# State space mixer of a two-layer trunk: its pieces in another order, convolution one chunk at a time, other engines for the first splits

## Chip, cores and metric

One core of a Trainium2 chip runs one launch of the kernel. The metric is the device time of a launch in microseconds (us), median of three runs; the profile is one further execution.

## What is computed

The reference is a trunk of two layers on 256 tokens of width 1024, in fp32. Layer 0 is a Mamba-2 mixer, layer 1 a retention; each is followed by a product-key expert network (the long part: 16384 expert rows of `peer_u` and `peer_v`) and a gated input embedding. Only the mixer of layer 0 is touched by the order of the change:

```python
proj = h @ w_in                                   # 1024 -> 2048 (z) + 3072 (x, B, C) + 32 (dt)
z = proj[..., :DI]
xbc = silu(causal_depthwise_conv(proj[..., DI:DI + 3072], conv_w, conv_b))   # 4 taps
dt = softplus(proj[..., DI + 3072:] + dt_bias)
# chunked scan: y[t] = sum_s exp(cum_t - cum_s) * (C_t . B_s) * dt_s * x_s, plus the state of the chunks before
y = (y + d_skip * xs) * silu(z)
y = rms_norm(y in 4 groups of 512, norm_g)
return y @ w_out                                  # 2048 -> 1024
```

## The kernel before

**Layout.** Activations are transposed: a chunk is 128 channels on the partitions by 256 tokens. Each weight tile (128 x 1024) is loaded by SP (`load`), cast to a high part on ACT (`wh`, L133) and subtracted to a low part (`wl`, L136) on DVE, or on POOL where `eng=pool` says so; a matmul step (`Acc.step`, L199) runs 16 matmuls with wh and then 8 with wl. `raws` has four buffers for loads, `wsp` two for each of wh and wl. `makers` holds the weights in order; `begin` issues the next load, `prepare` splits the oldest load, and `get` hands a step its weight, prepares the next one and issues one more load. `prepare(True)` (by `ahead` in the mixer, and in `finish`) emits the cast and keeps the subtraction for later; with `eager` set, `get` emits it one step before its use. So the DVE queue holds, step by step, one subtraction and then what the step's pieces ask for.

**Stages of the mixer.** (1) Eight steps for B and C (columns group 4), with the input's norm run beside them by the plan `FIRST_SSD`, one string of letters for each step: a is nine small row loads, q the squares, t the total, s the spread of the root, c and b small parameters, 0/1 the scaling of each half of the normalised input on DVE, h/H its split (ACT cast L187, DVE subtraction L188). (2) Eight steps for x chunks 0 to 7 (group 2), with the convolution of B and C beside them. (3) dt's 24 matmuls, then eight steps for x chunks 8 to 15 (group 3), with the convolution of chunks 0 to 7 and dt's softplus (`dt_a`, `dt_b`, `dt_c`) beside them. (4, 5) Sixteen steps for z, evacuated after every eight by `z_evac` (L786 ACT tanh, L787 DVE). (6) Sixteen steps of w_out, fed by the four normalised groups.

**Order of the work around the steps.** After step k a dense loop emits a written number of entries of the list `todo` (`fill`). `SSD_ORDER` writes them for stages 4 to 6, one group between bars for each step. cpN is a piece of the convolution of chunks 8 to 15 (`conv_piece`: first tap on ACT L598, three more taps on DVE L593 for two chunks at once, later the silu L603 of two chunks). x{tb}{q} transposes four chunks on PE and scales them on DVE (L678, L679); X and Y make the part across halves (DVE L698; PE L702, DVE L703); uN, eN, hN belong to a pair of heads: masks on ACT (L710), cumulative sums on PE with exp on ACT and the product on DVE (L716, L718, L720), and the output (PE L730, L732, DVE L734). aN multiplies a group by its gate and squares it (DVE L747, ACT L284, POOL L285, L286), bN sums it (PE L249, DVE L256, POOL L258, DVE L268), cN spreads the root and splits the group (PE L275, DVE L301, ACT L302, DVE L295). cbN is C times B under the causal mask (PE L685, DVE L687).

All engines work through their queues in the order written. PSUM: `acc` four banks for the steps' sums, `mis` two (tiles m: cb, e, dt, and each group's sums from b to c), `gps` two (tiles g: x, Y, h).

Of the kernel before, what the change touches and what calls it, by code (L numbers as in the profile page):

```python
# [18 lines left out]
P = 128  # L19
T = 256  # L20
D = 1024
# [10 lines left out]
    cp0 x00 x10 u0 | cp1 X0 e0 u1 | cp2 Y0 e1 x01 x11 | cp3 h0 u2 X1 | cp4 e2 h1 u3 Y1 | cp5 e3 h2 u4  # L32
    | cp6 e4 h3 u5 x02 x12 | cp7 e5 h4 u6 a0
    | e6 h5 u7 b0 X2 | e7 h6 u8 x03 x13 | c0 e8 h7 u9 Y2 | a1 e9 h8 u10 | e10 h9 u11 b1 | e11 h10 u12 X3 c1
    | e12 h11 u13 Y3 | e13 h12 u14 a2
    | e14 h13 u15 | b2 e15 h14 | h15 | c2 a3 | | b3 | c3 | | | | | | | | |
# [3 lines left out]
SSD_DT = "dt_a dt_b dt_c cb0 edge cb1 cb2 cb3".split()  # L40
# [6 lines left out]
FIRST_SSD = ('aq', 't', 'c', 's', '0h', '', '1H', 'b')  # L47
# [38 lines left out]
def trunk(ctx: ExitStack, tc: tile.TileContext, a, out, dbg=None, stop=None):  # L86
# [43 lines left out]
    def split_r(r, n=D, eng=None):  # L130
        wh = wsp.tile([P, D], F32R, name="wh")
        wl = wsp.tile([P, D], F32R, name="wl")
        act.copy(wh[:, :n], r[:, :n])  # L133

        def lo():
            (eng or dve).tensor_sub(wl[:, :n], r[:, :n], wh[:, :n].bitcast(F32))  # L136
            return wh, wl

        return lo

    makers, begun, ready = [], [], []
    eager = [False]

# [10 lines left out]

    def get(more=True):
        if not ready:
            prepare()
        v = ready.pop(0)
        if callable(v):
            v = v()  # L160
        if ready and callable(ready[0]) and eager[0]:
            ready[0] = ready[0]()
        if more and not ready:
            prepare()
        begin()
        return v

    def staged(r, n, eng):
        return lambda: split_r(r, n, eng)

    def weights(w, n0, n1, k0=0, k1=KD, eng=None):
        for k in range(k0, k1):
            makers.append(lambda k=k: staged(load(w[k * P:(k + 1) * P, n0:n1], n1 - n0), n1 - n0, eng))
# [230 lines left out]
    def x_load(i):  # L404
        for tb in range(2):
            c = slice(512 * i, 512 * i + 512)
            sp.dma_start(xts[tb][:, c], a["x"][0, tb * P:(tb + 1) * P, c])

    x_load(0)
# [11 lines left out]
    row_load(*ROWS1[0], act)  # L421

# [60 lines left out]
    def total0():  # L483
        st0.sums = Sums()
        st0.dg = st0.sums.diag(D, ss, act)

    def before0(k):
# [3 lines left out]
        for b in (2 * k, 2 * k + 1):  # L491
            st0.hi(2 * b)
            st0.hi(2 * b + 1)
            if b == 0:
                prepare()
                begin()
# [38 lines left out]
    for g in (4, 2, 3):  # L535
        for k in range(KD):
            weights(a["ssd_w_in"][0], g * D, (g + 1) * D, k, k + 1, eng=pool if g == 4 and k else None)
# [21 lines left out]
    def ssd(st):  # L559
# [27 lines left out]
        def conv(c):  # L587
            r = rawc[c // 8]
            for m in range(1, 4):
                for j in range(2):  # L590
# [11 lines left out]
        def conv_silu(c):  # L602
            act.activation(xbc[:, c:c + 2], xbc[:, c:c + 2], AF.Silu)  # L603
# [8 lines left out]
        def conv_piece(c0, i):  # L612
            if i in (1, 2, 3, 4):
                conv(c0 + 2 * i - 2)
            if i >= 4:
                conv_silu(c0 + 2 * i - 8)
# [6 lines left out]
        xs = []  # L623
        begin()
# [31 lines left out]
        def dt_b():  # L656
# [5 lines left out]
            dve.tensor_mul(f4, f[3], f[3])  # L662
            dve.tensor_scalar(f[5], f4, 1.0 / 15, None, op0=OP.mult)
# [75 lines left out]
        def ahead():  # L739

            if len(ready) < 2:
                prepare(True)

# [15 lines left out]

        cp = conv_pieces(8)  # L760
        names = {"dt_a": (dt_a,), "dt_b": (dt_b,), "dt_c": (dt_c,), "edge": (edge,)}
        for i in range(8):
            names[f"cp{i}"] = cp[i]
# [13 lines left out]
        for c, n in zip(conv_pieces(0), SSD_DT):  # L777
            todo.extend((c, names[n]))
        dense(xs, conv_evac(8), lambda k: 2)
# [10 lines left out]
        eager[0] = True  # L790
# [12 lines left out]
        eager[0] = False  # L803
# [694 lines left out]
```

## Time and profile before

| | us |
|---|---|
| time, median of 3 runs (lowest to highest) | 2169.11 (2167.49 to 2170.3) |
| the profiled execution | 2167.4 |
| its span | 2165.6 |
| PE busy in the span | 2119.3 |
| mixer of layer 0, start of the span to its last step | 251.3 |

The profile is read from the stage: a table of busy times by stretch shows where PE stood and where its clock was low; the timeline of PE names for each wait the engine that ended it; the timelines of DVE, ACT and POOL at that place show what stood ahead of it in that engine's queue.

### The profile page before, as it was taken

The page shows a single profiled execution, that of the slowest core. Times are in us where ns is not written, and L with a number is a line of the kernel's source. Part 1 is how long each engine was busy: PE and PEld are TensorE (multiplying, and loading weights), DVE is VectorE, ACT ScalarE, POOL GpSimd, SP SyncE. Part 2 cuts the span into 40 slices and gives each one's busy share as a digit, 9 for nine tenths or more (in the row PEclk, how much of TensorE's full clock was granted, in tenths as well). Part 3 has the DMA queues.
Part 4 walks back from the last instruction along what each step waited for, and adds up shares of the span by engine and source line. Part 5 has one row for each costly group of instructions (what it writes and reads, how often), then busy time and mean ns, then how long its engine had stood idle before and what let it go on. Part 6 is the DMA issues. An engine that isn't in the chain of part 4 may idle for free. (4 is left out here: it accounts for less than half of the span.)

```text
span 2165.6 us, 39617 instructions
## 1 busy us (share of the span) xinstructions
PE 2119.3 (98%) x15013; PEld 1965.6 (91%) x15013; DVE 1553.3 (72%) x2638; ACT 1229.1 (57%) x2149; POOL 786.7 (36%) x365
## 2 busy tenths in 40 slices
PE   8989999999999999999999999999999999999997
PEld 8988999999999888888898999999999998888887
DVE  6767678888999555555686456989799975555556
ACT  5666444448887444444554444445688864444445
POOL 3001168886777100000133224788777740000001
PEclk9989999999999999999999999999999999999999
DMA  5423577655555665566656456765555566666653
GB/s 184 149 69 108 185 196 189 179 138 158 157 157 157 203 193 193 193 192 194 198 175 185 135 159 182 192 187 150 156 151 158 154 184 194 194 194 193 194 188 120
DMA packets 219574, 370.24 MB, mean 171 GB/s; under 512 B 24240, under 2 KB 163192, under 8 KB 219384
## 3 DMA queue, kind: packets, MB, share of 16 engines
q1 hardware_dynamic: 219064, 367.19, 57.0%
q8 instruction: 117, 1.92, 0.4%
q14 instruction: 73, 0.60, 0.1%
q10 hardware_dynamic: 320, 0.53, 0.1%
HBM read 364.48 MB, written 1.05 MB: 169 GB/s over the span
## 5 line engine op out<-in xcount | busy, mean ns | idle before, releaser
L136 DVE TENSOR_TENSOR wl<-raw,wh 128x1024 fp32r<-128x1024 f32 x398 | 496.5, 1249 | 401.4 <-ACT wh L133 401.2
L133 ACT CAST wh<-raw 128x1024 fp32r<-128x1024 f32 x429 | 450.5, 1051 | 480.0 <-PE ps L1309 358.3
L528 POOL TENSOR_TENSOR wl<-raw,wh 128x1024 fp32r<-128x1024 f32 x256 | 618.4, 2417 | 201.3 <-ACT wh L525 183.8
L1283 PE MATMUL m<-X,wh 128*128 128x256 f32 x2048 | 508.6, 286 | 1.1 <-ACT wh L525 1.0
L1309 PE MATMUL ps<-wh,X 128*128 128x512 f32 x2048 | 507.0, 389 | 0.0
L1284 PE MATMUL m<-X,wh 128*128 128x256 f32 x2048 | 502.2, 283 | 0.0
L1309 PEld LDWEIGHTS ps<-wh,X 128*128 128x128 f32 x2048 | 384.2, 188 | 79.5
L1283 PEld LDWEIGHTS m<-X,wh 128*128 128x128 f32 x2048 | 392.5, 192 | 2.2 <-ACT wh L525 1.9
L1284 PEld LDWEIGHTS m<-X,wh 128*128 128x128 f32 x2048 | 392.7, 192 | 0.0
L199 PE MATMUL ps<-X,wh 128*128 128x256 f32 x2368 | 334.2, 291 | 6.9 <-ACT wh L133 4.2
L344 POOL TENSOR_TENSOR arena<-arena 128x512 f32<-128x512 f32 x15 | 24.1, 1607 | 817.3 <-ACT arena L342 808.3
L199 PEld LDWEIGHTS ps<-X,wh 128*128 128x128 f32 x2368 | 306.4, 196 | 13.1 <-ACT wh L133 5.2
L1287 PE MATMUL m<-X,wl 128*128 128x256 f32 x2048 | 288.1, 283 | 2.0 <-POOL wl L528 1.9
L525 ACT CAST wh<-raw 128x1024 fp32r<-128x1024 f32 x256 | 266.7, 1042 | 24.1 <-DVE raw L520 15.2
L1309 PE MATMUL ps<-wl,X 128*128 128x512 f32 x1024 | 274.7, 389 | 0.0
L1287 PEld LDWEIGHTS m<-X,wl 128*128 128x128 f32 x2048 | 264.0, 192 | 3.8 <-POOL wl L528 3.8
L1309 PEld LDWEIGHTS ps<-wl,X 128*128 128x128 f32 x1024 | 192.2, 188 | 39.9
L1223 ACT ACTIVATE arena<-m 128x256 f32<-128x256 f32 (+15 forms) x248 | 82.2, 331 | 228.3 <-PE m L1287 227.9
L520 DVE STREAM_TRANSPOSE raw<-raw 128x1024 f32<-128x1024 f32 x144 | 179.0, 1243 | 41.1 <-DMA raw<-in_peer_u 31.1
L199 PE MATMUL ps<-X,wl 128*128 128x256 f32 x1184 | 176.7, 286 | 5.7 <-DVE wl L136 3.5
L199 PEld LDWEIGHTS ps<-X,wl 128*128 128x128 f32 x1184 | 157.6, 194 | 7.9 <-DVE wl L136 4.3
L520 DVE STREAM_TRANSPOSE raw<-arena 128x1024 f32<-128x1024 f32 x112 | 138.0, 1235 | 30.0 <-POOL wl L528 26.5
(269 smaller groups left out, 1992.0 us busy)
## 6 DMA issues: line engine op xcount, KB each, us to landing
raw<-in_peer_v SPq DMA_DIRECT2D x256, 512.0 KB, 4.3
raw<-in_peer_u SPq DMA_DIRECT2D x576, 128.0 KB, 3.1
arena<-in_peer_u SPq DMA_DIRECT2D x448, 128.0 KB, 3.3
raw<-in_ret_w_in SPq DMA_DIRECT2D x48, 512.0 KB, 4.0
raw<-in_ssd_w_in SPq DMA_DIRECT2D x41, 512.0 KB, 3.8
raw<-in_peer_w_q SPq DMA_DIRECT2D x32, 512.0 KB, 4.5
raw<-in_ssd_w_out SPq DMA_DIRECT2D x16, 512.0 KB, 3.9
raw<-in_ple_gate SPq DMA_DIRECT2D x16, 512.0 KB, 4.5
```

The costliest lines, as they stand in the source:

```text
L133: act.copy(wh[:, :n], r[:, :n])
L136: (eng or dve).tensor_sub(wl[:, :n], r[:, :n], wh[:, :n].bitcast(F32))
L199: pe.matmul(self.t[n // 2][:, n % 2], w[:, n * P:(n + 1) * P], x, start=st, stop=sp_, skip_group_check=True)
L344: pool.tensor_add(self.sq[:, 0], self.sq[:, 0], self.sq[:, b])
L520: dve.transpose(t.rearrange("p (k b i) -> p b k i", k=8, b=4), r.rearrange("p (b k i) -> p b k i", k=8, b=4))
L525: act.copy(wh, t)
L528: pool.tensor_sub(wl, t, wh.bitcast(F32))
L1223: act.activation(H[:, i, st:], ps[:, st:], AF.Gelu)
L1283: pe.matmul(last, wh[:, s], xh, start=k == 0, stop=False)
L1284: pe.matmul(last, wh[:, s], xl, start=False, stop=False)
L1287: pe.matmul(last, wl[:, s], xh, start=False, stop=k == KD - 1)
L1309: pe.matmul(sums[b], h[:, tb * P:(tb + 1) * P], w[:, n * 512:(n + 1) * 512], start=i == 0 and p == 0, stop=i == P - 1 and p == 2)
```

## The change

Loads at the start: the first halves of x go out after the row of gains, one on SP and one on ACT's queue; two weights are begun before the second halves of x, and the `begin` inside `before0` goes. The first weight of group 4 is cast on DVE instead of ACT; of group 4 only the second weight has its subtraction on POOL (before: the second to the eighth). `total0` calls `ahead` first. `FIRST_SSD` has the split of the first half one step later, the second half's scaling together with b and its split at the end. `get` always emits a kept subtraction one step ahead, in all stages of the kernel.

In the convolution, pieces for chunks 0 to 15 are now separate entries: F (first tap, two chunks), v (three taps of one chunk), S (silu of four chunks). dt's softplus is cut in two (`dt_b`, then `dt_B` for the series). Stage 3 has its own list by step, `SSD_DT`; cb2 and cb3 move from stage 3 to stages 4 and 5. In `SSD_ORDER` x11, x12, x03, x13 and the a, b and c entries come at other steps.

```diff
 SSD_ORDER = """
-    cp0 x00 x10 u0 | cp1 X0 e0 u1 | cp2 Y0 e1 x01 x11 | cp3 h0 u2 X1 | cp4 e2 h1 u3 Y1 | cp5 e3 h2 u4
-    | cp6 e4 h3 u5 x02 x12 | cp7 e5 h4 u6 a0
-    | e6 h5 u7 b0 X2 | e7 h6 u8 x03 x13 | c0 e8 h7 u9 Y2 | a1 e9 h8 u10 | e10 h9 u11 b1 | e11 h10 u12 X3 c1
-    | e12 h11 u13 Y3 | e13 h12 u14 a2
-    | e14 h13 u15 | b2 e15 h14 | h15 | c2 a3 | | b3 | c3 | | | | | | | | |
+    S4 x00 x10 u0 F8 | X0 e0 u1 v8 F10 | Y0 e1 x01 v9 F12 | h0 u2 X1 v10 F14 | e2 h1 u3 Y1 v11 | e3 h2 u4 x11 v12 S8
+    | e4 h3 u5 x02 v13 | e5 h4 u6 v14 cb2
+    | e6 h5 u7 X2 x12 v15 | a0 e7 h6 u8 S12 | e8 h7 u9 Y2 | b0 e9 h8 u10 x03 | e10 h9 u11 x13 cb3 c0
+    | a1 e11 h10 u12 X3 | e12 h11 u13 Y3 | b1 e13 h12 u14
+    | e14 h13 u15 c1 | e15 h14 a2 | h15 | b2 | a3 | c2 | | b3 | c3 | | | | | | |
 """
...
-SSD_DT = "dt_a dt_b dt_c cb0 edge cb1 cb2 cb3".split()
+SSD_DT = """
+    F0 F2 dt_a | F4 v0 dt_b | F6 v1 dt_B | v2 dt_c | edge v3 | S0 v4 cb0 | v5 cb1 | v6 v7
+"""
+SSD_DT = [p.split() for p in SSD_DT.split("|")]
...
-FIRST_SSD = ('aq', 't', 'c', 's', '0h', '', '1H', 'b')
+FIRST_SSD = ('aq', 't', 'c', 's', '0', 'h', '1b', 'H')
...
-    def split_r(r, n=D, eng=None):
+    def split_r(r, n=D, eng=None, cast=None):
...
-        act.copy(wh[:, :n], r[:, :n])
+        (cast or act.copy)(wh[:, :n], r[:, :n])
...
+    def ahead():
+
+        if len(ready) < 2:
+            prepare(True)
...
-        if ready and callable(ready[0]) and eager[0]:
+        if ready and callable(ready[0]):
             ready[0] = ready[0]()
...
-            sp.dma_start(xts[tb][:, c], a["x"][0, tb * P:(tb + 1) * P, c])
-
-    x_load(0)
+            (act if i == 0 and tb else sp).dma_start(xts[tb][:, c], a["x"][0, tb * P:(tb + 1) * P, c])
...
     row_load(*ROWS1[0], act)
+    x_load(0)
...
     def total0():
+        ahead()
...
             if b == 0:
                 prepare()
-                begin()
...
-            weights(a["ssd_w_in"][0], g * D, (g + 1) * D, k, k + 1, eng=pool if g == 4 and k else None)
+            weights(a["ssd_w_in"][0], g * D, (g + 1) * D, k, k + 1, eng=pool if g == 4 and k == 1 else None,
+                    cast=dve.tensor_copy if g == 4 and k == 0 else None)
...
-        def conv(c):
+        def conv(c, n=2):
...
-                for j in range(2):
+                for j in range(n):
...
-            act.activation(xbc[:, c:c + 2], xbc[:, c:c + 2], AF.Silu)
+            act.activation(xbc[:, c:c + 4], xbc[:, c:c + 4], AF.Silu)
...
-            if i >= 4:
-                conv_silu(c0 + 2 * i - 8)
+            if i in (5, 7):
+                conv_silu(c0 + 2 * i - 10)
...
         xs = []
         begin()
+        begin()
         x_load(1)
...
+        def dt_series():
+            f4 = f[-1]
             dve.tensor_scalar(f[5], f4, 1.0 / 15, None, op0=OP.mult)
...
-        for c, n in zip(conv_pieces(0), SSD_DT):
-            todo.extend((c, names[n]))
-        dense(xs, conv_evac(8), lambda k: 2)
+        todo.extend(names[n] for part in SSD_DT for n in part)
+        dense(xs, conv_evac(8), lambda k: len(SSD_DT[k]))
```

## Rows read from the trace of the kernel before

**Rows 1.** The page: busy time of each engine, its share of the span, and its instructions.

```profile
PE 2119.3 (98%) x15013; PEld 1965.6 (91%) x15013; DVE 1553.3 (72%) x2638; ACT 1229.1 (57%) x2149; POOL 786.7 (36%) x365
```

**Rows 2.** Busy time of the engines by stretch: to the end of dt's matmuls, stage 3, stage 4 to its last step, that step, stage 5, stage 6, and all the rest. The columns are the stretch, its length, busy us (and instructions) of each engine, the mean granted clock, the DMA share and GB/s.

```profile
0.00:65.10 65.10, 56.88 (x430) 54.55 (x431) 41.68 (x75) 36.70 (x52) 20.98 (x15) 1.00 0.60 187
65.10:96.50 31.40, 29.45 (x225) 28.85 (x224) 25.33 (x58) 21.27 (x30) 0.00 (x0) 0.95 0.46 136
96.50:136.20 39.70, 35.91 (x285) 33.29 (x284) 29.81 (x53) 32.48 (x56) 0.00 (x0) 0.95 0.34 107
136.20:141.50 5.30, 5.30 (x39) 5.01 (x38) 3.79 (x5) 3.41 (x5) 0.00 (x0) 0.74 0.31 100
141.50:191.00 49.50, 46.25 (x367) 42.32 (x366) 34.02 (x64) 31.81 (x68) 5.66 (x6) 0.93 0.26 79
191.00:251.30 60.30, 57.03 (x464) 55.25 (x464) 35.55 (x57) 28.10 (x45) 7.36 (x7) 0.97 0.48 155
251.30:2165.60 1914.30, 1888.51 (x13218) 1746.35 (x13216) 1383.17 (x2331) 1075.36 (x1898) 752.67 (x337) 1.00 0.59 175
```

**Rows 3.** The timeline of PE up to 220 us, only the lines with a wait: start, length, line, operation, and in brackets the idle time before it and what ended it. The first line without a bracket is a run of 16 matmuls at the low clock.

```profile
8.26 3.78 PE L199 MATMUL ps<-X,wh 128*128 128x256 f32 x16 [1.64 <-ACT wh L133]
21.34 2.17 PE L199 MATMUL ps<-X,wh 128*128 128x256 f32 x16 [1.28 <-ACT wh L133]
23.87 1.22 PE L199 MATMUL ps<-X,wl 128*128 128x256 f32 x8 [0.36 <-POOL wl L136]
35.15 0.51 PE L199 MATMUL ps<-X,wl 128*128 128x256 f32 x2 [0.50 <-POOL wl L136]
79.46 1.22 PE L199 MATMUL ps<-X,wl 128*128 128x256 f32 x8 [1.95 <-DVE wl L136]
111.29 0.82 PE L678 MATMUL g<-ident,arena 128*128 128x128 f32 x4 [1.96 <-DVE arena L703]
111.76 3.61 PE L199 MATMUL ps<-X,wh 128*128 128x256 f32 x16
134.80 0.66 PE L678 MATMUL g<-ident,arena 128*128 128x128 f32 x4 [1.84 <-DVE arena L734]
149.88 1.02 PE L249 MATMUL m<-ones,arena 128*128 128x1 f32 x4 [2.85 <-POOL arena L286]
158.87 0.66 PE L678 MATMUL g<-ident,arena 128*128 128x128 f32 x4 [0.34 <-DVE arena L734]
214.39 1.21 PE L199 MATMUL ps<-X,wl 128*128 128x256 f32 x8 [1.17 <-DVE wl L136]
217.21 0.81 PE L249 MATMUL m<-ones,arena 128*128 128x1 f32 x4 [1.60 <-POOL arena L286]
```

**Rows 4.** Groups of DVE instructions up to 252 us, and the one of POOL's subtractions up to 70 us (lowest, median and highest ns): line, shapes, count, busy us and mean ns, idle time before.

```profile
L136 DVE TENSOR_TENSOR wl<-raw,wh 128x1024 fp32r<-128x1024 f32 x50 | 61.9, 1241 | 26.1 <-ACT wh L133 26.1
L787 DVE SCALAR_TENSOR_TENSOR arena<-arena,ps 128x512 f32<-128x512 f32 x8 | 5.3, 686 | 1.3 <-ACT arena L786 1.2
L136 POOL TENSOR_TENSOR wl<-raw,wh x8: 2389/2401/2996, 10.9 to 59.9; 128x1024 fp32r<-128x1024 f32 x8
```

**Rows 5.** Stage 1: two instructions of POOL from 16 to 20 us, and on DVE the scaling of the input's second half (four instructions), its split, and the evacuation of the four banks.

```profile
16.38 2.41 POOL L136 TENSOR_TENSOR wl<-raw,wh 128x1024 fp32r<-128x1024 f32 x1 [3.10 <-ACT wh L133]
18.89 0.73 POOL L258 TENSOR_TENSOR r<-r,mhalf 128x2 f32<-128x2 f32 x1
...
30.38 1.64 DVE L363 SCALAR_TENSOR_TENSOR arena<-hT,par,m 128x256 f32<-128x256 f32 x4
33.14 3.04 DVE L188 TENSOR_TENSOR X<-arena,X 128x1024 fp32r<-128x1024 f32 x1 [1.11 <-ACT X L187]
37.24 2.47 DVE L357 TENSOR_TENSOR arena<-ps,arena 128x512 f32<-128x512 f32 x4
```

**Rows 6.** Groups of ACT instructions up to 252 us.

```profile
L133 ACT CAST wh<-raw 128x1024 fp32r<-128x1024 f32 x59 | 61.4, 1043 | 35.1 <-PE ps L199 29.0 <-DVE wl L136 3.8 <-DMA raw<-in_ssd_w_in 1.3
L603 ACT ACT_TABLE_LOAD x7 | 9.0, 1283 | 0.1
L603 ACT ACTIVATE arena<-arena 128x512 f32<-128x512 f32 x12 | 7.6, 631 | 0.1
```

**Rows 7.** The DVE queue of stage 3 before the wait at 79.46, and of stage 4 before the wait at 111.29.

```profile
75.17 0.19 DVE L658 TENSOR_SCALAR arena<-arena 128x64 f32<-128x64 f32 x1
...
76.77 1.50 DVE L665 SCALAR_TENSOR_TENSOR arena<-arena,g 128x64 f32<-128x64 f32 x6
78.18 1.22 DVE L136 TENSOR_TENSOR wl<-raw,wh 128x1024 fp32r<-128x1024 f32 x1
...
108.19 2.44 DVE L593 SCALAR_TENSOR_TENSOR arena<-arena,par 128x255 f32<-128x255 f32 x6
110.55 0.68 DVE L703 TENSOR_TENSOR arena<-g,arena 128x512 f32<-128x512 f32 x1
```

**Rows 8.** Starts of steps on PE's timeline: two that follow each other in stage 2, and the second step of stage 3, whose first began at 65.1.

```profile
42.02 2.08 PE L199 MATMUL ps<-X,wh 128*128 128x256 f32 x16
...
44.90 2.08 PE L199 MATMUL ps<-X,wh 128*128 128x256 f32 x16
...
69.58 2.17 PE L199 MATMUL ps<-X,wh 128*128 128x256 f32 x16
```

More of the change, by code (lines that the diff above doesn't have):

```diff
@@ L141, in trunk @@
     makers, begun, ready = [], [], []
-    eager = [False]
     def begin():
@@ L166, in get, with staged, weights @@
         return v
-    def staged(r, n, eng):
-        return lambda: split_r(r, n, eng)
-    def weights(w, n0, n1, k0=0, k1=KD, eng=None):
+    def staged(r, *how):
+        return lambda: split_r(r, *how)
+    def weights(w, n0, n1, k0=0, k1=KD, eng=None, cast=None):
         for k in range(k0, k1):
-            makers.append(lambda k=k: staged(load(w[k * P:(k + 1) * P, n0:n1], n1 - n0), n1 - n0, eng))
+            makers.append(lambda k=k: staged(load(w[k * P:(k + 1) * P, n0:n1], n1 - n0), n1 - n0, eng, cast))
     todo = []
@@ L662, in dt_b @@
             dve.tensor_mul(f4, f[3], f[3])
+            f.append(f4)
+        def dt_series():
+            f4 = f[-1]
             dve.tensor_scalar(f[5], f4, 1.0 / 15, None, op0=OP.mult)
@@ L737, in ssd @@
         gn = {}
-        def ahead():
-            if len(ready) < 2:
-                prepare(True)
         def gn_square(g):
@@ L758, in gn_scale @@
             gn[g] = norm(gs.spread(dg), [y[:, 4 * g + i] for i in range(4)], COL["ssd_norm"] + 4 * g)
[L760 to L763, printed above, removed]
+        names = {"dt_a": (dt_a,), "dt_b": (dt_b,), "dt_B": (dt_series,), "dt_c": (dt_c,), "edge": (edge,)}
+        for c in range(16):
+            names[f"v{c}"] = (conv, c, 1)
+            names[f"F{c}"] = (conv_first, c)
+            names[f"S{c}"] = (conv_silu, c)
         for g in range(4):
@@ L788, in z_evac @@
             return f
-        eager[0] = True
         dense(xs, z_evac(0), lambda k: len(SSD_ORDER[k]))
@@ L802, in ssd @@
                 fill(len(SSD_ORDER[16 + 4 * g + i]) if g < 2 else 2)
-        eager[0] = False
         return finish(s, COL["ffn_norm"])
```

## Prediction

> **What bounds the kernel now.** I read the page first, then the table by stretch, then the waits on PE's timeline, and last, at each wait, the queue of the engine that ended it. PE is busy 2119.3 of 2165.6 us [rows 1], so only its idle time and its low clock can be won. The table by stretch [rows 2] says where both lie. Behind 251.3 us the code is the same and the clock 1.00. Ahead of it PE stood 65.10 - 56.88 = 8.2 us up to dt's end, then 1.95, 3.8, 0, 3.25 and 3.3 us: 20.5 in all. Of the first 8.2 us, 2.14 are waits named below and nearly all the rest lies ahead of the first matmul with a weight at 8.26 [rows 3], where the loads set the time. The clock column gives the rest: a stretch of length L at mean clock c does (1 - c)L less work than at 2.4 GHz, so 0.05 x 31.4 = 1.6, 0.05 x 39.7 = 2.0, 0.26 x 5.3 = 1.4, 0.07 x 49.5 = 3.5 and 0.03 x 60.3 = 1.8: 10.3 us. The low stretches are at 1.2 GHz: 16 matmuls take 3.61 us behind the wait at 111.29 where they take 2.17 at 21.34 [rows 3]. Such a stretch came behind the waits of 1.95, 1.96, 1.84, 2.85 and 1.60 us, and none came behind that of 1.28. I count five, so one costs 10.3 / 5 = 2.1 us.
>
> What is to be won therefore stands in one list, the waits [rows 3]: 1.28 + 0.36 + 0.50 in stage 1, 1.95 in stage 3, 1.96 and 1.84 in stage 4, 2.85 + 0.34 in stage 5, 1.17 + 1.60 in stage 6: 13.85 us, and 10.3 of clock behind them.
>
> **The change part by part.** The sum is made against the profiled execution, 2167.4 us; its span is 2165.6, so 1.8 lies around it. The median of the runs shown is 1.7 above it, which I add at the end.
>
> *Start.* The first matmul waits for wh at 8.26 [rows 3], cast on ACT among the input's own activations. The first weight's load now goes out one issue (0.4 us) earlier, beside one half of x on the other queue; the bytes that must land first are the same. Its cast moves to DVE, which no row shows. Bounds: 0.5 us (half of the subtraction of that shape, 1.24 [rows 4]) to that 1.24, against ACT's 1.04 [rows 6]. I take a value near the middle and a gain of 0.5; ends 0 and 1.2. VectorE: DVE Perf Modes of the Trainium skill (section "The perf-mode tier table") puts an fp32 copy within SBUF at twice the rate of a two-input operation; by it the cast would be near 0.6 us, an estimate, and the gain about 0.7. No run here shows it yet.
>
> *Stage 1.* The 1.28 us at 21.34 come from a chain: POOL's subtraction 2.41 stands ahead of the root's 0.73 [rows 5], the diagonal on ACT waits for the root, and the next weight's cast stands behind the diagonal. Now POOL is free there and `ahead` puts the cast ahead of the diagonal: 1.28 goes. The low parts come 1.24 instead of 2.40 after the cast [rows 4], so 0.36 and 0.50 go too. Six subtractions come to DVE, 6 x 1.24 = 7.4 us; the table of the stretch has DVE idle 23.4 of 65.1 [rows 2], yet the end of the stage is dense. From the sixth weight on DVE does four subtractions of weights (4.9), two scalings (1.64 each), one split (1.2), parameters (0.4) and the evacuation of four banks (2.47) [rows 5], 12.3 us, starting when that weight is cast, near 24.9: it ends at 37.2 where PE is done at about 35.2, so stage 2 gets its banks late, and more so than before. I give back 0.5. Rows show what POOL costs DVE: the input's split takes 3.04 beside a subtraction of POOL [rows 5], where the same shape takes 1.24 [rows 4]. SBUF — State Buffer of the Trainium skill (section "Who interferes with whom") says that a DVE instruction with two SBUF inputs and a GpSimd one that reads SBUF lock each other out for their whole length. By that rule the split falls to 1.24, as in my sum; at the old 3.04 the give-back would be 2.3. Stage 2 is bound by PE and gives nothing. Net with the start: 0.5 + 2.14 - 0.5 = 2.1.
>
> *Stage 3.* In one step DVE held the subtraction 1.22, taps of two chunks 2.44, and dt's reciprocal and series (3.0, from 75.17 to 78.18) [rows 7]: 6.7 us where a step of PE takes 2.88 [rows 8], and the next subtraction came 1.95 late. Now the steps hold 1.2 + 1.2 + 1.3, then 1.2 + 1.2 + 1.7, then 1.2 + 1.2 + 1.0. I walked the two queues. DVE is without a gap from 6.5 us behind the start of the stage; the fourth subtraction is 0.5 late, and dt_c ends 11.2 us of DVE work later, at 17.7, where PE, after five steps of 2.88, dt_a's 1.6 (the second step begins 4.48 behind the first [rows 8]) and that 0.5, reaches `edge` at 16.45: 1.25 idle. Behind that cb0 and cb1 leave it time. So 1.95 + 1.6 of clock go and 1.75 come. cb2 and cb3 (0.8 us of PE each) only move.
>
> *Stage 4.* 111.29: x11 waited for a bank that DVE frees at L703, behind taps of two chunks [rows 7]. x11 is three steps later now and v stands last in its step: 1.96 and the clock's 2.0 go. 134.80 was the same for x12, behind L734: 1.84 and 1.4 go. ACT has silus of four chunks (priced between 0.63 and 2 x 0.63, I take 1.05, the cast of that shape [rows 6]) and by the order written six fewer table loads of 1.28 up to 252 us, off PE's path. New: the subtraction and v13 stand ahead of the four L787 (0.69 each [rows 4]); in the walk the last bank is free at 40.0 after the stage's start while PE needs it at 38.8, and I charge 1.35.
>
> *Stage 5.* b0 came one step behind a0 and waited 2.85 for POOL; it comes two steps behind now. 2.85 + 0.34 and 3.5 go. New: ACT waits for DVE's gate product in a0 and a1 and makes the next masks late: 0.8 at e8 and 1.1 at e12. ScalarE: Activation LUTs of the Trainium skill (section "What ACT_TABLE_LOAD costs") adds a drain of 1.38 us to each load of 1.28. The group here shows 1.283 each and 0.1 of idle before all seven [rows 6], so I keep that. By the page the silu's load and e8's would make e8 2.8 later, and the time would be near 2155.
>
> *Stage 6.* a3 and b3 stand three steps apart instead of two, and c2 no longer shares a step with a3: 1.17 + 1.60 + 1.8 go, nothing new.
>
> *Elsewhere.* `get` emits the kept subtraction a step earlier behind each of the four `finish`. It only changes places with a low part of the input that is due two steps later: 0, bounds 0.5 either way each.
>
> *Sum.* Goes: 0.5 + 13.85 + 10.3 = 24.65. Comes: 0.5 + 1.75 + 1.35 + 1.9 = 5.5. Net 19.15. Whether the clock falls behind a wait of 1.25 or 1.35 the rows leave open (1.28 and 1.60 are the nearest); I charge one such stretch, 2.1. That makes 17.05: 2167.4 - 17.05 = 2150.35, and 1.7 on top 2152.
>
> **Rivals.** (1) *DVE stays the bound.* For it: its queue is full from 6.5 us on in stage 3 and nearly so in stage 4. If four of my new waits are each followed by 1.2 GHz (3 x 2.1 more) and grow by 0.7 each, 9 us are lost: 2161, with 2158 to 2165 around it. Against it: the taps stand last in a step, behind what PE waits for. (2) *All covered*: no new wait, no low clock; 24.65 and a start better by 0.7: 2144. (3) *Slower, by the bank that a sum holds.* From b to c a group's sums keep one of the two m banks, so that e9, e10 and cb3 (b0 to c0) and e13, e14 (b1 to c1) pass one after the other through the second; before it was one e each time. Each pass is matmuls, exp, and DVE's product. My walk has 0.1 us of wait, since a step lies between two e. If DVE or ACT is late by w at each of the five, PE loses 5(w + 2.1); from w = 1.7 on the whole 19 are gone, and at w = 2.6 it is 2173. Against it: DVE's product stands ahead of the other pieces. (4) *No gain*: each cured wait is met by the next late engine, as where the wait at 158.87 follows that at 149.88 [rows 3]; 2165 to 2171, I say 2168.
>
> **How the numbers follow.** Forecast 0.60 (2152; own range 2146 to 2158), rival 1 0.20, rival 2 0.06, rival 3 0.08, rival 4 0.06. The range of 8 in 10 takes the forecast's own, rival 2's end and most of rival 1: 2144 to 2163. About 0.2% (4 us) is what a measurement of this kernel can tell from no change. Faster: 0.60 + 0.20 + 0.06 = 0.86; same 0.06; slower 0.08.
>
> **What would show it.** Right: no PE wait on L678, on L249 or for a POOL subtraction; first matmul near 7.8; clock 0.97 or more in every stretch of the mixer; w_out's first step near 174 to 177 instead of 191, its end near 233 instead of 251; small waits at `edge`, behind z's evacuation, and at e8 and e12 for ACT's masks. Wrong: waits on DVE L136 in stages 3 to 5 with 1.2 GHz behind them (rival 1), waits of PE at L716 or L685 on DVE L720 (rival 3), or a longer stretch behind the mixer.

## The result, and the profile after

The changed kernel takes 2146.98 us (median of five executions, 2146.21 to 2147.86) against 2169.11 (five, 2166.85 to 2170.3): a ratio of 0.9904, 95% interval 0.9891 to 0.9916. The forecast was 2152, its range 2144 to 2163. The profiled execution takes 2147.86 against 2167.4: 19.5 less where the sum had 17.05 (its span, 2145.3, is 20.3 shorter).

The page of the changed kernel, its line of busy times, answers to [rows 1]:

```profile
PE 2112.3 (98%) x15013; PEld 1959.3 (91%) x15013; DVE 1559.6 (73%) x2645; ACT 1218.8 (57%) x2136; POOL 772.1 (36%) x359
```

PE did the same 15013 matmuls in 7 us less busy time, so the other 13 were idle time. The table by stretch, cut at the same events as [rows 2] (end of dt's matmuls, of stages 3 and 4, the step behind, stages 5 and 6, the rest), but for the last cut: 230.5 answers to 252.3 before, one group of matmuls behind the 251.3 of [rows 2].

```profile
0.00:60.40 60.40, 54.62 (x431) 53.56 (x432) 45.42 (x82) 35.42 (x49) 6.94 (x9) 1.00 0.64 202
60.40:90.30 29.90, 28.38 (x216) 27.70 (x215) 23.51 (x50) 17.39 (x25) 0.00 (x0) 0.94 0.48 142
90.30:130.30 40.00, 39.52 (x325) 36.24 (x323) 33.12 (x55) 29.84 (x56) 0.00 (x0) 1.00 0.37 111
130.30:135.40 5.10, 5.00 (x43) 4.51 (x43) 5.03 (x9) 3.59 (x10) 0.00 (x0) 1.00 0.17 67
135.40:174.00 38.60, 38.60 (x326) 35.35 (x323) 30.78 (x56) 28.41 (x56) 4.75 (x5) 1.00 0.30 95
174.00:230.50 56.50, 55.99 (x472) 54.48 (x470) 39.47 (x70) 30.45 (x49) 8.09 (x8) 1.00 0.55 174
230.50:2145.30 1914.80, 1890.16 (x13212) 1747.41 (x13212) 1382.23 (x2329) 1073.73 (x1897) 752.27 (x337) 1.00 0.59 175
```

Read the length first, then PE's busy time against it, then the clock (the eighth figure). From 90.3 to 230.5 PE stands 1.1 us in 140 and the clock is 1.00; only stage 3 still has both idle time (1.5) and a low clock (0.94). The waits of PE's timeline in the mixer, with the first run of weight matmuls and the low run of stage 3 (no brackets), answer to [rows 3]; a wait of 0.34 at 230.5 is left out:

```profile
6.28 1.75 PE L459 MATMUL g<-ident,arena 128*128 128x128 f32 x7 [2.35 <-DMA arena<-in_x]
7.74 3.34 PE L206 MATMUL ps<-X,wh 128*128 128x256 f32 x16
...
76.15 1.22 PE L206 MATMUL ps<-X,wl 128*128 128x256 f32 x8 [0.58 <-DVE wl L139]
78.31 0.41 PE L705 MATMUL m<-arena 128*128 128x32 f32 x2 [0.94 <-DVE arena L685]
78.89 3.57 PE L206 MATMUL ps<-X,wh 128*128 128x256 f32 x16
130.27 2.06 PE L206 MATMUL ps<-X,wh 128*128 128x256 f32 x12 [0.31 <-DVE arena L795]
```

The whole list of 13.85 us in [rows 3] is gone, and 0.58 + 0.94 + 0.31 have come. By stretch, lengths of before minus those of after, which add up to the 20.3:

| stretch | forecast | measured |
|---|---|---|
| start and stage 1, to the first matmul of stage 2 (at 38.06 before, 33.53 after) | 2.1 | 4.5 |
| stage 2 | 0 | 0.2 |
| stage 3, less the two cb moved out of it (1.1) | -0.3 | 0.4 |
| stages 4 to 6 (96.5 to 252.3 before, 90.3 to 230.5 after), plus these 1.1 | 15.2 | 16.7 |
| the rest | 0 | -1.5 |

(Forecast: stage 3 is 1.95 + 1.6 - 1.75, less the low-clock stretch of 2.1 that the sum charged once; stages 4 to 6 are 5.85 + 4.79 + 4.57. Measured: on PE's timeline of before, cb2 takes from 92.41 to 92.98 and cb3 from 95.94 to 96.51, 0.57 each, where the prediction had 0.8.)

### The profile page after: what moved, and what is told of

Read it like the earlier page. It is cut to its first block, busy times and chain, and to the rows that moved or that the text cites. A ratio compares the mean times of both kernels' runs of the same rounds, so it can differ in the third digit from the quotient of the medians.

```text
span 2145.3 us, 39601 instructions
## 1 busy us (share of the span) xinstructions
PE 2112.3 (98%) x15013; PEld 1959.3 (91%) x15013; DVE 1559.6 (73%) x2645; ACT 1218.8 (57%) x2136; POOL 772.1 (36%) x359
## 3 DMA queue, kind: packets, MB, share of 16 engines
HBM read 364.48 MB, written 1.05 MB: 170 GB/s over the span
## 4 chain that ended last, share of the span: by engine, by line
PE 44%; DVE 2%; issue 1%; POOL 1%; ACT 1%; DMA 1%; SPq 0%; DVEq 0%; POOLq 0%; ACTq 0%
PE ps L1315 16%; PE ps L206 7%; PE m L1289 5%; PE m L1293 5%; PE m L1290 5%; PE ps L913 2%; PE g L1209 1%; DMA raw<-in_peer_u 1%; PE g L1017 0%; DVE wl L139 0%; POOL wl L139 0%; DVE raw L527 0%; PE g L865 0%; POOL wl L535 0%; SPq L524 0%
## 5 line engine op out<-in xcount | busy, mean ns | idle before, releaser
L139 DVE TENSOR_TENSOR wl<-raw,wh 128x1024 fp32r<-128x1024 f32 x404 | 503.6, 1248 | 397.2 <-ACT wh L136 396.9
L206 PEld LDWEIGHTS ps<-X,wh 128*128 128x128 f32 x2368 | 302.0, 194 | 9.5 <-DVE arena L364 1.9
```

The lines of the kernel that those rows point to most:

```text
L206: pe.matmul(self.t[n // 2][:, n % 2], w[:, n * P:(n + 1) * P], x, start=st, stop=sp_, skip_group_check=True)
```

## Experiments

Twelve kernels ran, each timed beside the kernel before. The theory under test: the gain is the waits and the clock behind them, cured by the new places of the pieces, and it adds up stage by stage. The rivals: that one part did it all, or that a wait cured only moves to the next late engine. The medians of small undoings lie within 0.65 us of the changed kernel's, so these are read from the trace by stretch. A trace is one execution. In the eleven that have the first halves of x on two queues (SP's and ACT's, as in the change), x's transposes start between 6.28 and 7.58 and the first weight matmul 1.46 or 1.47 behind them, and the first step differs in length too. From the second step to stage 2, though, it is 20.86 to 20.88 in every trace but those of before (24.11), e1 and e2, so the front's parts are read from there.

**e1: POOL's subtractions back in stage 1.**

```diff
-            weights(..., eng=pool if g == 4 and k == 1 else None,
+            weights(..., eng=pool if g == 4 and k else None,
```

> The changed kernel with one part undone: the low parts of the second to the eighth weight of stage 1 are again subtracted on POOL. Theory (a POOL subtraction takes 2.40 us against 1.22 on DVE and lies ahead of the root and beside DVE's split): the waits on POOL's low part come back, 0.4 and 0.5 us, and the split of the input takes 2 to 3 us again, so stage 2 begins 1 to 2.5 us later: 2148 to 2149.5. Rival (the six subtractions fill DVE's queue at the end of stage 1, as the prediction charged): nothing is lost, 2147 within 0.5.

2146.74 (2145.85 to 2149.32). From the second step to stage 2 it takes 21.87 instead of 20.86; one wait of those of [rows 3] is back, in PE's timeline, and stage 2's first matmuls follow:

```profile
32.80 0.50 PE L206 MATMUL ps<-X,wl 128*128 128x256 f32 x2 [0.31 <-POOL wl L139]
...
35.28 2.46 PE L206 MATMUL ps<-X,wh 128*128 128x256 f32 x16
```

These take 2.46 where they take 3.06 in the changed kernel, so of the 1.0 only 0.4 is left at stage 3 (48.17 from the second step, against 47.76). So moving the subtractions off POOL is worth 1.0 at stage 2 and 0.4 behind it. The split of the input shows what they cost DVE, on its timeline: first beside three subtractions of POOL (24.61 to 32.74), then with POOL idle:

```profile
27.21 3.27 DVE L195 TENSOR_TENSOR X<-arena,X 128x1024 fp32r<-128x1024 f32 x1 [1.93 <-ACT X L194]
...
36.14 1.21 DVE L195 TENSOR_TENSOR X<-arena,X 128x1024 fp32r<-128x1024 f32 x1
```

**e2: no `ahead` in the total.**

```diff
     def total0():
-        ahead()
```

> The changed kernel without the call of ahead in total0, so that the fourth weight's cast stands behind the diagonal on ACT again. Theory (ACT's order makes that wait): the diagonal ends at 19.85 us in the changed kernel's trace, the cast at 20.9, and the fourth step, which now begins at 18.37, begins 2.5 us later: 2149.5, or up to 2151.5 if a stretch at 1.2 GHz follows. Rival (POOL's subtraction ahead of the root made the wait, and it is gone): 2147 within 0.5.

2146.99 (2146.65 to 2150.55). The wait at the fourth step is back with the length it had, in PE's timeline:

```profile
20.85 2.18 PE L206 MATMUL ps<-X,wh 128*128 128x256 f32 x16 [1.28 <-ACT wh L136]
```

From the second step to stage 2 the kernel takes 22.42, 1.56 more than with `ahead`, so this line is worth 1.6 of the front's 4.5. The median doesn't show it: in this execution stage 3 has its two waits again, 0.57 and 0.94, but the clock behind them stays at 1.00. That is a line of the table by stretch, of e2 first and of the changed kernel below:

```profile
60.00:96.00 36.00, 34.42 (x278) 33.54 (x277) 29.30 (x59) 21.38 (x30) 0.00 (x0) 1.00 0.49 149
```

```profile
60.00:96.00 36.00, 34.41 (x265) 33.53 (x265) 29.26 (x60) 20.31 (x30) 0.00 (x0) 0.95 0.45 136
```

In 36 us, 0.05 of the clock is 1.8 us. Of the nine profiled executions that have this pair of waits (0.56 to 0.58, then 0.94 or 0.95), four show 0.95 here and five 1.00.

**e3: the kept subtraction emitted one step ahead in the mixer alone,** and behind it as before (`eager` set for the mixer and reset at its end).

> The changed kernel with the kept subtraction emitted a step early in the mixer alone, and as before behind it. Theory (the 1.5 us that the rest of the kernel takes longer in the changed kernel's profile is a stretch at 1.2 GHz that falls behind a wait of the retention by chance): 2147 within 0.5. Rival (the early subtraction costs the rest 1.5 us): 2145.5.

2146.34 (2144.80 to 2147.39). Outside the mixer the edit is worth nothing that can be measured, as the sum had it. At the mixer's end this execution waits 0.66 for ACT's split and 0.39 for `hT`, where the changed kernel has the 0.34.

**e4: the dt row ahead of the taps in stage 3.**

```diff
-    F0 F2 dt_a | F4 v0 dt_b | F6 v1 dt_B | v2 dt_c | edge v3 | S0 v4 cb0 | v5 cb1 | v6 v7
+    F0 F2 dt_a | F4 dt_b v0 | F6 dt_B | dt_c v1 | edge v2 v3 | S0 v4 cb0 | v5 cb1 | v6 v7
```

> The changed kernel with the pieces of dt ahead of the taps in stage 3: v0 behind dt_b, v1 behind dt_c, v2 and v3 behind edge. Theory (the low part at 76.15 and edge wait for DVE work that PE doesn't need yet): the waits of 0.58 and 0.94 us go and so does the stretch at 1.2 GHz behind them, about 1.7 us: 2144 to 2145. Rival (DVE is full, so the taps that are now late hold ACT at the silu S4 in the first step of stage 4, and the masks behind it): the same time reappears there, 2146.5 to 2148.

2146.34 (2145.03 to 2146.43). Both waits of stage 3 are gone, and the clock is 1.00 from 60 to 96 (as in five of the nine executions with these waits, see e2); two others have come at the end of the stage:

```profile
84.92 0.50 PE L206 MATMUL ps<-X,wl 128*128 128x256 f32 x2 [0.62 <-DVE wl L139]
...
88.55 2.06 PE L206 MATMUL ps<-X,wh 128*128 128x256 f32 x12 [0.50 <-DVE arena L617]
```

So the rival was nearer, though the time comes back sooner than it had it: DVE has the same work, and its order decides where PE meets it. The second wait names a copy (L617) that ACT can do as well.

**e5: both first halves of x on SP's queue again.**

```diff
-            (act if i == 0 and tb else sp).dma_start(xts[tb][:, c], ...)
+            sp.dma_start(xts[tb][:, c], ...)
```

> One part undone: both first halves of the input go on SP's queue again, in the order of the changed kernel; ACT's queue carries none of them. Theory, that the second queue is what delays x (its first half landed at 4.86 us in the kernel before, at 6.28 to 7.58 in the runs of the changed one so far): x lands near 4.9, the first weight matmul starts at 7.0 to 7.3 instead of 7.74, and the time falls by 0.4 to 0.7, to about 2146.4. Rival, that the bytes of x and of the first weight's halves have to come through the same 16 engines whichever queue names them: first weight matmul at 7.7 again, time 2147.

2146.47 (2144.18 to 2147.95). Both theories missed. x lands earlier (the transposes start at 5.40 instead of 6.28), but the weight behind it on the same queue lands later. DVE's cast of the first weight and PE's first step, from their timelines:

```profile
7.76 0.69 DVE L136 CAST wh<-raw 128x1024 fp32r<-128x1024 f32 x1 [3.53 <-DMA raw<-in_ssd_w_in]
```

```profile
8.60 3.75 PE L206 MATMUL ps<-X,wh 128*128 128x256 f32 x16 [1.44 <-DVE wh L136]
12.15 1.91 PE L206 MATMUL ps<-X,wl 128*128 128x256 f32 x8
```

The cast starts at 7.76 instead of 6.08, the first step at 8.60 instead of 7.74, and its low matmuls take 1.91 instead of 1.12: the clock is still low. Stage 2 starts at 35.80 instead of 33.53. So the second queue is worth 0.9 at the first matmul and 2.3 at stage 2. (e8, on one queue too, has 8.61 and 35.73; the eight traces with the change's front have stage 2 between 33.30 and 34.32, so 1.4 to 2.5 is the range.) The median doesn't show it; in this execution too, stage 3's clock stayed at 1.00.

**e6: the front alone.** The kernel before with the loads, the cast, the subtractions, `ahead` and `FIRST_SSD` of the change, and the kept subtraction one step ahead throughout.

> The kernel before with the front part of the change alone: the order of the first loads and of the first products' pieces, the first weight's cast on DVE, the subtractions moved from POOL to DVE, and two weights prepared ahead; the convolution, the silus, the schedules of stages 3 to 6 are those of the kernel before. Theory, that every microsecond won ahead of PE in stages 0 and 1 stays won, since PE is the bound behind it: stage 2 starts at about 33.5 instead of 38.03, the waits of stages 3 to 6 are those of the kernel before (1.95, 1.96, 1.84, 2.85, 1.17, 1.60), and the time falls by 4.3 to 4.8, to about 2164.6. Rival, that the later waits were waits for DVE, POOL and DMA work that doesn't come earlier: they grow by what the front gave, and the time is 2167 to 2169.

2164.47 (2161.75 to 2168.95, eleven executions); the ratio, 0.9993 (0.9983 to 1.0003), can't be told from 1. The trace can: stage 2 starts at 33.38, 4.7 earlier, and the waits behind are those of [rows 3] to 0.02 us:

```profile
74.50 1.93 PE L204 MATMUL ps<-X,wl 128*128 128x256 f32 x8 [1.95 <-DVE wl L136]
...
106.38 0.66 PE L685 MATMUL g<-ident,arena 128*128 128x128 f32 x4 [1.96 <-DVE arena L710]
106.79 2.15 PE L204 MATMUL ps<-X,wh 128*128 128x256 f32 x16
...
142.20 0.61 PE L254 MATMUL m<-ones,arena 128*128 128x1 f32 x4 [2.84 <-POOL arena L291]
```

The later waits don't grow by what the front gave: it is 4.9 ahead at the start of stage 4 (91.59 against 96.51), and the stages add up. By the mixer's end it is 6.6 ahead (245.72 against 252.31), and that needn't be the front's doing: behind the bank waits of stage 4, 1.96 and 1.83, the matmuls here run at 2.4 GHz (16 in 2.15, where before shows 3.61), which makes 1.5 each. The times set a bound, too: their interval leaves the front 3.7 us at most.

**e7: x11 back in the second step of stage 4.**

```diff
-    ... | Y0 e1 x01 v9 F12 | ... | e3 h2 u4 x11 v12 S8
+    ... | Y0 e1 x01 x11 v9 F12 | ... | e3 h2 u4 v12 S8
```

> One part undone: the last group of taps (x11) stands again behind x01 in the second step of stage 4's row instead of in its last step. Theory, that the group has to wait for the bank that Y0's product on DVE frees, and that this product stands behind the cast work of its step: a wait of 1.5 to 2 at the second step's end near 103, perhaps with a stretch at the lower clock behind it (1.5 more), and 2148.5 to 2150. Rival, that with the silus masked and one chunk per step the bank is long free: no wait, and 2147.

2149.37 (2146.47 to 2150.35). The wait for the bank is back. PE's line, and DVE's queue ahead of it:

```profile
105.28 0.65 PE L691 MATMUL g<-ident,arena 128*128 128x128 f32 x4 [1.52 <-DVE arena L716]
```

```profile
103.40 1.23 DVE L139 TENSOR_TENSOR wl<-raw,wh 128x1024 fp32r<-128x1024 f32 x1 [0.98 <-ACT wh L136]
104.55 0.68 DVE L716 TENSOR_TENSOR arena<-g,arena 128x512 f32<-128x512 f32 x1
```

Y0's product (L716) frees the bank, and a subtraction that waits for a cast stands ahead of it. Moving x11 is worth 2.4 by the medians, even with the taps out of the way.

**e8: the dt row first, all four evacuations of stage 3 on ACT, x on SP.** (What left stage 3 besides is the taps v7, not a silu.)

```diff
-    F0 F2 dt_a | F4 v0 dt_b | F6 v1 dt_B | v2 dt_c | edge v3 | S0 v4 cb0 | v5 cb1 | v6 v7
+    F0 F2 dt_a | F4 dt_b v0 | F6 dt_B | dt_c v1 | edge v2 | v3 cb0 | S0 v4 cb1 | v5 v6
-    S4 x00 x10 u0 F8 | X0 e0 u1 v8 F10 |
+    x00 x10 u0 F8 v7 | S4 X0 e0 u1 v8 F10 |
-                (dve.tensor_copy if b % 2 else act.copy)(rawc[...], ps)
+                (dve.tensor_copy if b % 2 and c0 == 0 else act.copy)(rawc[...], ps)
```

> A version put together from what the first four runs showed: x on SP, the dt row ahead of the silus in stage 3 (its two waits of 0.58 and 0.94 were gone in that run), one silu fewer in stage 3 and one more ahead of stage 4's decays, and stage 3's four evacuations all on ACT, so that the waits of 0.62 and 0.50 that the dt row alone brought (for a weight's subtraction and for an evacuation, both on DVE) go too. Theory, that DVE's order around the dt row is what PE waits for: no wait over 0.3 from 60 to 96, and 2143.5 to 2144.5. Rival, that DVE is full over the whole of stages 3 and 4 and the wait only moves to stage 4's first steps: 2146 to 2147.

2145.24 (2143.95 to 2146.26). No wait from 60 to 96, although its first matmul came at 8.61 as in e5. DVE wasn't full: the wait didn't move on. Which of the order, the two copies and v7 was needed wasn't tried one by one.

**e9: the squares and sums of the first and last group as close as before.**

```diff
-    | ... | a0 e7 h6 u8 S12 | e8 h7 u9 Y2 | b0 e9 h8 u10 x03 | ...
+    | ... | e7 h6 u8 S12 a0 | e8 h7 u9 b0 Y2 | e9 h8 u10 x03 | ...
-    | ... | b2 | a3 | c2 | | b3 | c3 | ...
+    | ... | b2 | | c2 a3 | | b3 | c3 | ...
```

> One part undone: the squares and the sum of the first and of the last group of y stand as close as in the kernel before (a0 last in its step and b0 in the next one; c2 and a3 in one step and b3 two steps later). Theory, that the distance is what cured the waits: a0's squares come behind the silu and the masks on ACT and then two operations on POOL (2.1), so PE waits about 2.6 to 3.0 for b0 near 146, and 1.6 for b3 near 207 with 1.2 for a subtraction ahead of it, each of the larger ones perhaps with a stretch at the lower clock (about 1.5): 2152 to 2156. Rival, that the silus and taps taken out of the way did it: no wait over 0.5 at b0 or b3, and 2147.

2157.55 (2153.6 to 2163.17): 10.6 slower by the medians, nearly half of the gain undone by the places of three entries (a0, b0, a3). PE's timeline, with the low matmuls behind each wait:

```profile
148.09 1.01 PE L256 MATMUL m<-ones,arena 128*128 128x1 f32 x4 [2.57 <-POOL arena L293]
...
150.03 4.40 PE L206 MATMUL ps<-X,wh 128*128 128x256 f32 x16
...
209.86 1.21 PE L206 MATMUL ps<-X,wl 128*128 128x256 f32 x8 [1.17 <-DVE wl L139]
212.68 1.01 PE L256 MATMUL m<-ones,arena 128*128 128x1 f32 x4 [1.60 <-POOL arena L293]
213.55 3.76 PE L206 MATMUL ps<-X,wh 128*128 128x256 f32 x16
```

The three waits are those of stages 5 and 6 in [rows 3]. The table by stretch has the clock at 0.93 over 49.5 us and 0.94 over 60: 3.5 and 3.6. With 5.3 of waits that is 12.4; from stage 4's start to the mixer's end the trace is 11.7 longer. What held PE is on ACT's timeline, where the squares (L291) stand behind the table load, the silu and a cast, since a0 is last in its step here; so the first wait holds a0's place within the step as well as its distance from b0:

```profile
141.55 1.28 ACT L611 ACT_TABLE_LOAD   x1
142.85 1.06 ACT L611 ACTIVATE arena<-arena 128x1024 f32<-128x1024 f32 x1
143.81 1.03 ACT L136 CAST wh<-raw 128x1024 fp32r<-128x1024 f32 x1
144.75 1.14 ACT L291 ACTIVATE arena<-arena 128x512 f32<-128x512 f32 x2
145.91 1.28 ACT L731 ACT_TABLE_LOAD   x1
147.20 0.58 ACT L731 ACTIVATE m<-m 128x512 f32<-128x512 f32 x1
```

**e10: the taps of two chunks at once in stage 4.** v8 with v9, up to v14 with v15, one pair a step.

> One part undone, in stage 4 alone: the three taps run for two chunks at once again (8 with 9, 10 with 11, 12 with 13, 14 with 15, one pair a step) instead of one chunk a step. By the queue of DVE in the changed kernel the subtraction that ends at 108.86 there, and which PE needs at 109.27, would come 1.9 later; the following ones have slack of 2.5 and more. Theory, that the size of the lump is what counts: one wait of 1.5 to 1.9 near 109 for a weight's subtraction, perhaps with a stretch at the lower clock behind it (1.5), and 2148.5 to 2150.5. Rival, that the amount over the stage counts and not the lump, since DVE has gaps there: no wait over 0.5, and 2147.

2146.35 (2145.04 to 2146.54). One wait of 0.41 at 109.11, and stages 4 to 6 as long as in the changed kernel (140.10 against 140.19). The lump was smaller than I took it: two chunks at once cost DVE 2.44 (first row), one chunk 1.51 (second row, of the changed kernel), so what stands behind a pair comes 0.93 later and not the 1.9 expected, and no later wait shows it.

```profile
105.48 2.44 DVE L601 SCALAR_TENSOR_TENSOR arena<-arena,par 128x255 f32<-128x255 f32 x6
```

```profile
100.78 1.51 DVE L601 SCALAR_TENSOR_TENSOR arena<-arena,par 128x255 f32<-128x255 f32 x3
```

In stage 4, one chunk per step is worth nothing by itself.

**e11: silus of two chunks, and the second weight behind the second halves of x.**

```diff
-        begin()
-        begin()
-        x_load(1)
+        begin()
+        x_load(1)
+        begin()
-            act.activation(xbc[:, c:c + 4], xbc[:, c:c + 4], AF.Silu)
+            act.activation(xbc[:, c:c + 2], xbc[:, c:c + 2], AF.Silu)
-    ... S0 v4 cb0 | ... X0 e0 u1 v8 F10 | ... | e4 h3 u5 x02 v13 | ... e8 h7 u9 Y2
+    ... S0 v4 S2 cb0 | ... X0 e0 u1 S6 v8 F10 | ... | e4 h3 u5 S10 x02 v13 | ... e8 h7 u9 S14 Y2
```

> Two small parts undone, in places far apart, to be read from the trace by stretch: the silus are of two chunks again, with six more loads of ACT's table up to the end of stage 5 (three of them and their returns stand between two exps), and the second weight is loaded behind the second halves of the input instead of ahead of them. Theory: the loads of the table (1.28 each) stand behind masks and cost PE nothing, or under 0.5; the second weight comes 1 to 1.5 later and its first matmul waits for that, so the second step starts near 14 instead of 12.67 and stage 2 starts 1 later: 2148. Rival one, that ACT is the next bound in stages 4 and 5: waits for exp of 0.5 to 1.5 at e1, e5 and e9, together 2 to 4, and 2150 to 2152. Rival two, that the order of the loads at the start is indifferent since the bytes of both must come first: stage 2 starts where it did, 2147.

2150.60 (2149.2 to 2151.8). The second step starts at 12.30 and stage 2 at 33.17, not later than in the changed kernel: so rival two holds for the front, the order of these loads is indifferent. The silus cost more than the theory had, but not at an exp: at 102.14 PE waits 0.65 for a cast that stands behind a table load and a silu, and then

```profile
125.44 0.69 PE L691 MATMUL g<-ident,arena 128*128 128x128 f32 x2 [3.29 <-ACT arena L611]
```

where x02's transposes need the silu, which on ACT stands behind a table load for the exp, four masks and its own load:

```profile
120.39 1.28 ACT L731 ACT_TABLE_LOAD   x1
121.69 0.58 ACT L731 ACTIVATE m<-m 128x512 f32<-128x512 f32 x1
122.18 1.27 ACT L723 ACTIVATE arena<-arena 128x128 f32<-128x128 f32 x4
123.47 1.28 ACT L611 ACT_TABLE_LOAD   x1
124.76 0.63 ACT L611 ACTIVATE arena<-arena 128x512 f32<-128x512 f32 x1
```

This holds for the places that I gave the second silus; other places weren't tried.

**e12: e8 with x's second block on ACT's queue, as in the changed kernel.**

> The version of the run before this one (dt row ahead of the silus, all evacuations of stage 3 on ACT) with the first half of x's second block on ACT's queue again, as in the changed kernel. Theory: the two parts add up; the first weight matmul starts at 7.7 to 7.9 instead of 8.61 and stage 2 at 33.5 instead of 35.73, no wait over 0.35 in stages 3 to 6, and the time is 2.2 below that run: 2142.5 to 2143.5. Rival, that the earlier start only meets the next late engine in stage 3: waits of 1 to 2 come back between 60 and 96, 2145.

2143.60 (2142.71 to 2145.73), a ratio to the kernel before of 0.9885, 0.9871 to 0.9899: the lowest median here, 1.6 below e8, though the two intervals overlap (e8: 0.9888 to 0.9918). The first weight matmul starts at 7.93, stage 2 at 33.46, and stage 3 has neither idle time nor low clock:

```profile
60.00:96.00 36.00, 36.00 (x297) 35.56 (x296) 29.85 (x60) 25.38 (x37) 0.00 (x0) 1.00 0.52 152
```

Of the front's 2.3 all is there in stage 5 (126.28 against e8's 128.55), and 1.05 at the mixer's end (227.69 against 228.74), where PE waits 1.06 for ACT's split; the clock is 0.97 from 191 to 251.

## Why the prediction was right, and where it was off

**The frame held.** The list of waits went as a whole, the low clock with it except in stage 3, and DVE, the suspected next bound, let PE wait 1.8 us up to the mixer's last steps. e9 shows the largest term by itself, e7 the one at 111.29, e2 the 1.28, e6 that the stages add up in the trace. The move of x12 (1.84) wasn't undone by itself. Rival 1 falls: no chain of DVE waits from stage 4 on. Rival 3 falls: no wait at the matmuls of e or cb, whose banks it had short. Rival 4 falls with the result. Rival 2 was nearer than its 0.06: at 2144 it lies 3 below the median, the forecast 5 above.

**Start: right in the number, by luck.** The cast takes 0.69, between the bounds of 0.5 and 1.24 (half of the subtraction's 1.24 is 0.62, not 0.5), and PE starts 0.52 earlier. It was taken near the middle and is near the lower end. But the cast no longer sets the start. The cast before, on ACT's timeline, and the cast after, on DVE's:

```profile
7.16 1.04 ACT L133 CAST wh<-raw 128x1024 fp32r<-128x1024 f32 x1 [0.52 <-DMA raw<-in_ssd_w_in]
```

```profile
6.08 0.69 DVE L136 CAST wh<-raw 128x1024 fp32r<-128x1024 f32 x1 [1.72 <-DMA raw<-in_ssd_w_in]
```

The weight is there 1.1 us earlier than before and x 1.4 later (its transposes start at 6.28 instead of 4.86), and the first weight matmul follows the transposes without a wait for `wh`. In the ten other traces with two queues it starts at 7.82 to 9.04, so 7.74 is the earliest of eleven.

VectorE: DVE Perf Modes of the Trainium skill (section "The perf-mode tier table") has such a copy at twice the rate of a two-input operation; the trace agrees, 0.69 against 1.23 for the subtraction. But the sentence "the bytes that must land first are the same" hid what moved: e5 shows that the two queues are what brings the weight in by 6.08.

**Stage 1: the step that failed.** The step is "2.14 - 0.5", and both terms were mis-sized; with the start, 4.5 came in place of 2.1. The give-back didn't come: DVE's queue has no gap from 24.51 to 34.99, as I drew it, but three subtractions of weights stand in it and not four; the four evacuations start at 32.59, while PE is at the last banks, and the first matmuls of stage 2 take 3.06 where they took 3.15 at 38.06 before. Moreover the waits were worth more than their brackets: from the second step to the fourth the kernel takes 5.82 instead of 7.39, 1.57 for a bracket of 1.28, and from the fourth to stage 2 15.04 instead of 16.72, 1.68 for 0.36 + 0.50. e2 says the same: 1.56 for a bracket of 1.28. These 3.25 come in every trace that has the change's front. The first step is 0.76 shorter, since its low clock ended sooner, and that is chance: in the eight traces with this front it takes 4.47 to 5.53 (5.69 in the one of before), and stage 2 starts 3.7 to 4.8 earlier than before.

**The split beside POOL: right.** Without POOL's subtraction the split takes 1.23 where it took 3.04 [rows 5], and e1, with them back, shows 3.27.

```profile
27.27 1.23 DVE L195 TENSOR_TENSOR X<-arena,X 128x1024 fp32r<-128x1024 f32 x1
```

**Stage 3: right, to the wait.** Forecast 0.5 for a subtraction and 1.25 at `edge`; measured 0.58 and 0.94, and one low stretch where one was charged. The walk of the two queues did that, with two errors that partly cancel: it had one chunk's taps at 1.2, half of two chunks' 2.44, and they take 1.51 (e10), and it had PE at `edge` 16.45 behind the start of the stage, where PE comes at 16.9; dt_c ends at 17.9 instead of 17.7. One sign of being right failed, a clock of 0.97 or more in every stretch: it is 0.94 here, as the low stretch that the sum itself charged would have it. e4 and e8 show that what the walk found was an order, not a bound: e8, with dt's row first, two copies given to ACT and v7 a step later, has neither wait.

**Stage 4: right in kind.** The two bank waits went; z's evacuation has 0.31 where 1.35 was charged. The 3.4 us of clock behind the two waits, though, are what this one execution of the kernel before lost: e6 has the same waits without them.

**Stage 5: the mechanism was there, its size was off.** ACT makes the masks for e8 and e12 late as said, but PE lost 0 and 0.3 where 0.8 and 1.1 were charged. The masks (L723, four) on ACT and the matmuls that take them (L729) on PE, for e8 and e12:

```profile
142.11 1.26 ACT L723 ACTIVATE arena<-arena 128x128 f32<-128x128 f32 x4
...
165.26 1.26 ACT L723 ACTIVATE arena<-arena 128x128 f32<-128x128 f32 x4
```

```profile
143.12 1.06 PE L729 MATMUL m<-arena 128*128 128x128 f32 x8
...
165.73 1.34 PE L729 MATMUL m<-arena 128*128 128x128 f32 x8
```

PE starts e8 at 143.12, before the fourth mask is done (143.37), and e12 at 165.73 (166.52), where the group takes 1.34 instead of 1.06. The sum waited for the last mask. The silu behind e8's masks makes e8's exp late (147.05), but no wait of PE follows from it. ScalarE: Activation LUTs of the Trainium skill (section "What ACT_TABLE_LOAD costs") adds a drain of 1.38 to each load; no run here shows one: in e9's rows the exp starts 1.29 behind the start of its load.

**Stages 5 and 6, the clock.** Charged 5.3 for two stretches; e9, which brings the waits back, shows 7.1. That a low stretch comes behind every wait of 1.60 or more was read too firmly, on both sides: 0.57 + 0.94 bring one in four of nine executions, 1.96 and 1.83 bring none in e6, and the retention's wait of 1.79 (at 1255.8 before, at 1234.8 after) is followed by matmuls at 2.4 GHz in the one and at 1.2 in the other. This last stretch cost nothing: before, PE waits 1.19 for ACT a step later, and from the step ahead of the wait of 1.79 to the next wait for `hT` it takes 58.2 in both (1250.70 to 1308.94, 1229.71 to 1287.93).

**The rest of the kernel** was to be the same and is 1.5 longer. The two traces differ in the first part of the two expert networks, from PE's wait of 0.66 for a subtraction of POOL (at 280.24 and 1337.65 after) to its wait of 0.83 for DVE (504.23 and 1562.37): 223.24 and 223.61 before, 223.99 and 224.72 after. The twelve other kernels have 223.05 to 224.14 and 223.58 to 225.00 there, and e3, which has the code of before behind the mixer, 223.59 and 224.64. So it goes with the execution and not with the edit; its cause stays open. The whole rest varies between 1913.2 and 1916.1 over the other kernels.

**What did the work.** By undoing: the distance of the sums, with a0's place in its step, 10.6; the front 4.5 in the trace (3.7 to 4.8 over eight traces; the times of e6 leave it open and allow 3.7 at most), the silus of four with their places 3.6, x11's place 2.4. Nothing that could be measured by themselves: one chunk per step in stage 4, the second weight ahead of x's rest, the subtraction ahead elsewhere. The parts overlap and needn't add up to 22.

## What to carry to other kernels

A chain over several engines (DVE, ACT, POOL) that PE waits for was cured here by one more step of distance, at no cost where a buffer is free: the places of three entries of a list were worth 10.6 us of 22. Walk the queues for the waits that will come, but count a wait from the operand that is used first, not from the last one made. Judge edits of 1 us by the distances between steps in the trace, where a wait of 1.28 shows as 1.6; the total hides them. And look first at which distances are the same in every trace: 20.87 from the second step to stage 2 is, the first step and the clock behind a wait are not.

## What the runs showed of the hardware that was not expected

- The granted clock behind the same waits differs between executions: 0.95 or 1.00 over the same 36 us (1.8 us) in stage 3; low behind 1.96 and 1.84 before, and not behind 1.96 and 1.83 in e6 (1.5 us each). The medians of four or five executions here didn't settle a difference of 1.
- Three dependent tap operations of one chunk take 1.51 on DVE, six of two chunks taken in turn 2.44: 0.50 against 0.41 each.
- Both halves of x and the first weight on one queue (e5, e8): the weight's cast starts at 7.76 and 7.77 and x's transposes at 5.40 and 5.08. With one half of x on a second queue (eleven traces): 5.96 to 6.83, and 6.28 to 7.58.
- A DVE subtraction of 128x1024 takes 1.21 to 1.23 by itself and 3.27 beside POOL's subtractions of the same shape, which take 2.7 each there instead of 2.4 (e1: three in 8.13).
